# FFN pairs: a fixed matmul order, sums of weight blocks on GpSimd, and two more wide pairs

## The chip, the cores and the metric

The kernel runs on one core of one Trainium2 chip. The metric is the device time of one execution in microseconds; the times shown are those of separate runs. The profile is taken in an execution of its own, and its span goes from the first to the last instruction of the program.

In the profile PE is TensorE (matmuls), PEld its loads of the stationary operand, DVE is VectorE, ACT ScalarE, POOL GpSimd and SP SyncE (which issues DMAs). A line such as L410 is line 410 of the kernel.

## The reference

One layer of an encoder over 512 tokens of width 1024: a half-step SwiGLU FFN, a mixing stage of two attention branches, and a second half-step FFN. Each has an RMSNorm before and after it. All of it is in float32.

```python
def _swiglu(x, w_gate, w_up, w_down):
    return (jax.nn.silu(x @ w_gate) * (x @ w_up)) @ w_down

f = _swiglu(_rmsnorm(x, ffn1_pre_g[l]), ffn1_w_gate[l], ffn1_w_up[l], ffn1_w_down[l])
x = x + 0.5 * _rmsnorm(f, ffn1_post_g[l])
...
f = _swiglu(_rmsnorm(x, ffn2_pre_g[l]), ffn2_w_gate[l], ffn2_w_up[l], ffn2_w_down[l])
x = x + 0.5 * _rmsnorm(f, ffn2_post_g[l])
```

The hidden width of an FFN is 2816, that is 22 tiles of 128 features (`NF = 22`). Only the two FFNs are touched by the change.

## The kernel before

**Precision.** A float32 product is made of three matmuls in the faster type float32r. Each operand is split into a high part (a cast on ACT, L113) and a low part (what is left, a subtraction on DVE, L114); high x high, high x low and low x high are added in PSUM (`mm3`, L204 to L206).

**Pairs.** An FFN works through its 22 hidden tiles in order. Each is a pair: a gate product and an up product of the normed input with a block of weights. The first two pairs (`STD`) are done in the plain way (`proj_into`). The other 20 go through `seven`, a Strassen-like scheme with seven block products instead of eight. The 1024 input features and the 512 tokens are both cut in halves, and gate and up weights take the place of the second dimension of blocks. So each pair j has seven products, numbered 1 to 7, of a block of weights 128 features wide with 256 tokens. The tokens' side (`mv`) is formed once for an FFN by `combined`; the weights' side is formed for each pair.

**Blocks of weights.** `load_blocks` issues a pair's loads: on SP plain ones, on GpSimd's queue two that add in the DMA (t1, which is up + gate, at L404, and t3 at L405). `sums_of` then forms two more blocks: t2 = t1 + w11 (L410), and t4 from t2 and another block (L412 for the first four pairs, which have it loaded, L415 for the others). `split_block` splits a block into high and low. `ready(j + 1, i)` calls these for the next pair between the products of this one, and past the last pair it takes steps of the down projection instead (`lead`, and `far` through `get`). The first four pairs (`EARLY`) have their products 1 and 2 done ahead, in `first_products`.

**One turn of the loop** over j (L485 on), as written: product 1 of pair j into a bank q; then 7 of pair j - 1 (q) and 5 of pair j (p); then 2 (r) and 6 (q) of pair j, 4 of pair j - 1 (q) and 3 of pair j (p). Between them ACT copies a bank before it is added to again (L494 after product 1, L514 after 5, L523 after 6, L527 after 7 and 4) and DVE combines the copies with later sums (L505 and L506 for 7 less 5, L520 for product 2, L528, L535 and L536), until `use7` forms silu(gate) x up (L636, L645, L646).

**Wide products.** In a narrow product each of the four blocks of 128 input features takes three matmuls over 256 tokens (`mm3`). In a wide one the tokens' high and low parts lie side by side, so the weights' high part is multiplied with both at once in one matmul over 512 columns (L461), and the low part with the high tokens over 256 (L464). The two halves of the 512 columns must then be added, so the copies and sums behind it work on 512 columns, or are one more. `run` issues the first halves (L461) of all products of a group and then their second halves (L464). Which pairs may be wide is `state["wide"]`: in the first FFN pairs 4 to 17 of 0 to 19, in the second all. Product 1 is narrow in every pair, and in the first four pairs only 5 and 3 can be wide.

**What sets the order.** The kernel is built through a planner, which simulates the engines and gives each engine a fixed list; dependences, written order and priorities go into it. So the order on an engine need not be the written one. Where the code wants the written order it says so: at the end of `block_kernel` a loop goes over ranges of the program (`ordered` for PE, ACT and DVE together, `pool` with the engines named in each entry) and chains all instructions of an engine in a range. The pair loop was in no such range for PE. The down projection (`rest`) chains GpSimd's instructions from its start on.

**Rooms.** Blocks and sums live in 38 rooms of 128 x 512 (`unit`), split blocks in 12 of 128 x 1024 (`wp`), PSUM results in 8 banks. A load waits until its room is free.

Of the kernel before, what the change touches and what calls it, by code (L numbers as in the profile page):

```python
# [16 lines left out]
ALU = mybir.AluOpType  # L17
# [7 lines left out]
NF = 2816 // P  # L25
# [10 lines left out]
STD = 2  # L36
# [10 lines left out]
def block_kernel(ctx, tc, x, gains, weights, rpb_near, rpb_all, alibi0, alibi12, out):  # L47
    nc = tc.nc
# [12 lines left out]
    def unit(dt=F32, name="u"):  # L61
        return up.tile([P, 512], dt, tag="u", name=name)
# [57 lines left out]
    state = {"used": False, "next": 0, "take": 0, "stop": EARLY + 2 * STD, "ahead": lambda: None}  # L120
    ordered = []
    pool = []
# [65 lines left out]
    def mark():  # L188
        return len(nc.cur_bb.bb.instructions)
# [199 lines left out]
    def load_blocks(n0, j):  # L389

        w11, t1, t3 = unit(name="w11"), unit(name="t1"), unit(name="t3")
        gate, up = (n0 + j, n0 + EARLY + 2 * STD + j) if j < EARLY else [n0 + 2 * STD + 2 * j + i for i in range(2)]
        nc.sync.dma_start(t1, weights[up][:, :512])
        nc.sync.dma_start(t3, weights[up][:, :512])
        raw = {3: w11, 5: t1, 7: t3}
        if j < EARLY:
            raw[4] = unit(name="t4")
            nc.sync.dma_start(raw[4], weights[gate][:, 512:])
        else:
            r = wp.tile([P, PIECE], F32, tag="raw", name="raw", bufs=2)  # L400
            nc.sync.dma_start(r, weights[gate])
            raw[1], raw[2] = r[:, :512], r[:, 512:]
        nc.sync.dma_start(w11, weights[up][:, 512:])
        nc.gpsimd.dma_start(t1, weights[gate][:, :512], accum_op=ALU.add)  # L404
        nc.gpsimd.dma_start(t3, weights[up][:, 512:], accum_op=ALU.add)  # L405
        return raw

    def sums_of(raw):
        raw[6] = unit(name="t2")
        nc.vector.tensor_tensor(raw[6], raw[5], raw[3], op=ALU.add)  # L410
        if 4 in raw:
            nc.vector.tensor_tensor(raw[4], raw[6], raw[4], op=ALU.add)  # L412
        else:
            raw[4] = unit(name="t4")
            nc.vector.tensor_tensor(raw[4], raw[6], raw[2], op=ALU.add)  # L415

    def split_block(raw):
        w = wp.tile([P, PIECE], F32R, tag="w", name="w")
        split(w[:, :512], w[:, 512:], raw)
        return w  # L420

    def seven(use, mv, n_pairs, n0, behind, far, lead, raws, early, put, pin):

        blocks = {}
        o = {}

        def get(j):
            if j < n_pairs and j > 2:
                raws[j] = load_blocks(n0, j)
            if j >= n_pairs - 1:
                behind(far)

        def ready(j, i):
            if j < n_pairs:
                if j and loads:
                    loads.popleft()()  # L440
                if i == 1:
                    sums_of(raws[j])
                if j >= EARLY or i not in (1, 2):
                    blocks[j, i] = split_block(raws[j].pop(i))
            else:
                behind(lead)

        def product(j, i, key, start):
            if start:
                o[key, j] = bank(key)  # L450
            w = blocks.pop((j, i))
            high = [w[:, k * P:(k + 1) * P] for k in range(4)]
            low = [w[:, 512 + k * P:512 + (k + 1) * P] for k in range(4)]
            acc = o[key, j][:, :256]
            if i not in WIDE or j not in state["wide"] or (key in "qr" and j < EARLY):
                for k in range(4):
                    mm3(acc, high[k], low[k], *mv[i][k][:2], start and k == 0, k == 3, skip_group_check=True)
                return
            for k in range(4):
                to = shaped(o[key, j], mv[i][k][2])  # L460
                nc.tensor.matmul(to, high[k], mv[i][k][2], start=start and k == 0, stop=False, skip_group_check=True)  # L461
            yield
            for k in range(4):
                nc.tensor.matmul(acc, low[k], mv[i][k][0], start=False, stop=k == 3, skip_group_check=True)  # L464

        def run(*products):
            products = [product(*p) for p in products]
            for _ in range(2):
                for p in products:
                    next(p, None)  # L470

        def full(j):
            return j in state["wide"] and j >= EARLY

        res = {}
        get(0)
        get(1)
        blocks[0, 5] = split_block(raws[0][5])
        ready(0, 1)
        raws[0].pop(5)  # L480
        for i in (6, 3, 7, 4):
            ready(0, i)
            if i == 3:
                put()
        for j in range(n_pairs + 1):  # L485
            now, was = j < n_pairs, j > 0
            get(j + 2)
            if now:
                if j < EARLY:
                    o["q", j], g = early[j]  # L490
                else:
                    run((j, 1, "q", True))
                    g = unit(name="g")
                    nc.scalar.copy(g[:, :256], o["q", j][:, :256])  # L494
                u = unit(name="up")
                res[j] = g, u, unit(name="p5") if j in state["wide"] else u[:, 256:]
            ready(j + 1, 1)
            if pin and j == 0:
                pool.append((pin, mark(), (mybir.EngineType.DVE,)))
            run(*[(j - 1, 7, "q", False)] * was, *[(j, 5, "p", True)] * now)  # L500
            if was:
                g0, u0, s0 = res.pop(j - 1)
                q0 = o["q", j - 1]
                if full(j - 1):
                    nc.vector.tensor_tensor(s0, s0, q0, op=ALU.subtract)  # L505
                    nc.vector.tensor_tensor(u0[:, 256:], s0[:, :256], s0[:, 256:], op=ALU.add)  # L506
                else:
                    nc.vector.tensor_tensor(u0[:, 256:], s0[:, :256], q0[:, :256], op=ALU.subtract)
                if j - 1 in state["wide"] and not full(j - 1):
                    nc.vector.tensor_tensor(u0[:, 256:], u0[:, 256:], s0[:, 256:], op=ALU.add)  # L510
            ready(j + 1, 5)
            if now:
                p = o["p", j]
                nc.scalar.copy(res[j][2], p if j in state["wide"] else p[:, :256])  # L514
            ready(j + 1, 2)
            two = now and j >= EARLY
            run(*[(j, 2, "r", True)] * two, *[(j, 6, "q", False)] * now, *[(j - 1, 4, "q", False)] * was, *[(j, 3, "p", False)] * now)
            if two:
                for part in range(1 + full(j)):
                    nc.vector.tensor_tensor(g[:, :256], g[:, :256], o["r", j][:, part * 256:part * 256 + 256], op=ALU.add)  # L520
            ready(j + 1, 6)
            if now:
                nc.scalar.copy(u if full(j) else u[:, :256], o["q", j] if full(j) else o["q", j][:, :256])  # L523
            ready(j + 1, 3)
            if was:
                if full(j - 1):
                    nc.scalar.copy(g0[:, 256:], q0[:, 256:])  # L527
                    nc.vector.tensor_tensor(g0[:, 256:], q0[:, :256], g0[:, 256:], op=ALU.add)  # L528
                    use(j - 1, g0, u0, g0[:, 256:])
                else:  # L530
                    use(j - 1, g0, u0, q0[:, :256])
            ready(j + 1, 7)
            if now:
                if full(j):
                    nc.vector.tensor_tensor(u, p, u, op=ALU.subtract)  # L535
                    nc.vector.tensor_tensor(u[:, :256], u[:, :256], u[:, 256:], op=ALU.add)  # L536
                else:
                    nc.vector.tensor_tensor(u[:, :256], p[:, :256], u[:, :256], op=ALU.subtract)
                if j in state["wide"] and not full(j):
                    nc.vector.tensor_tensor(u[:, :256], p[:, 256:], u[:, :256], op=ALU.add)  # L540
            ready(j + 1, 4)

    def first_of_next():
        return [n for n in sorted(spread) if n >= state["next"]][:SPREAD]
# [72 lines left out]
    def ffn(g, store, src):  # L617
# [31 lines left out]
        raws = {}  # L649
# [27 lines left out]

        far, lead, rest = down(m, after, duos, hidden, g_post, g_pre, store, src)
        state["next"] = state["take"] = after + 2 * m + 2
        state["wide"] = range(NF - STD) if store else range(4, NF - STD - 2)  # L680
        seven(use7, mv, NF - STD, n0, lambda q: [f() for f in q.popleft()], far, lead, raws, early, put, pin)
        rest()

# [869 lines left out]
    raws = []  # L1553
# [9 lines left out]
    for n in range(2, 4):  # L1563
        raw = wp.tile([P, PIECE], F32, tag="raw", name="raw", bufs=2)
# [233 lines left out]
```

## Time and profile before

| | us |
|---|---|
| median of 3 runs | 1072.0 |
| lowest and highest run | 1071.46, 1072.08 |
| the profiled execution | 1071.59 |
| its span | 1069.8 |

| stage, by the timeline | us from the span's start |
|---|---|
| pairs of the first FFN (`seven`) | about 40 to 232 |
| down projection of the first FFN | about 225 to 339 |
| mixing stage | about 339 to 740 |
| pairs of the second FFN | about 766 to 963 |
| down projection of the second FFN and the output | about 951 to 1070 |

The page's first part has each engine's busy time, its share of the span and its instructions. The windows view gives each engine's busy time in a stretch (with the number of instructions), the clock granted to PE and the load of the DMA engines. The timeline lists one engine's instructions: start, duration, then in brackets the idle time before it and what ended that. The groups by line give busy time in all, mean ns of one, and idle time before them.

### The profile page before, as it was taken

The page shows a single profiled execution, that of the slowest core. Times are in us where ns is not written, and L with a number is a line of the kernel's source. Part 1 is how long each engine was busy: PE and PEld are TensorE (multiplying, and loading weights), DVE is VectorE, ACT ScalarE, POOL GpSimd, SP SyncE. Part 2 cuts the span into 40 slices and gives each one's busy share as a digit, 9 for nine tenths or more (in the row PEclk, how much of TensorE's full clock was granted, in tenths as well). Part 3 has the DMA queues.
Part 4 walks back from the last instruction along what each step waited for, and adds up shares of the span by engine and source line. Part 5 has one row for each costly group of instructions (what it writes and reads, how often), then busy time and mean ns, then how long its engine had stood idle before and what let it go on. Part 6 is the DMA issues. An engine that isn't in the chain of part 4 may idle for free.

```text
span 1069.8 us, 17141 instructions
## 1 busy us (share of the span) xinstructions
PE 1060.3 (99%) x5939; PEld 924.1 (86%) x5939; DVE 871.1 (81%) x1698; ACT 655.1 (61%) x1348; POOL 191.2 (18%) x253
## 2 busy tenths in 40 slices
PE   9999999999999999999999999999999999999997
PEld 7899888998888988888988888889899888887886
DVE  7989999989987566777777644777999989999985
ACT  7656657576684665567766641366656556667671
POOL 4112111124334000000000001143301111123321
PEclk9999999999999999999999999999999999999999
DMA  9889988779993444322232239585938767869952
GB/s 338 190 218 239 228 196 214 197 182 269 255 305 112 164 162 148 118 79 60 81 104 81 79 126 300 150 198 192 285 81 206 175 180 197 210 208 229 219 197 79
DMA packets 98026, 193.95 MB, mean 181 GB/s; under 512 B 24337, under 2 KB 26897, under 8 KB 97938
## 3 DMA queue, kind: packets, MB, share of 16 engines
q1 hardware_dynamic: 69760, 138.37, 38.8%
q0 software_dynamic: 25488, 54.01, 28.1%
q8 instruction: 47, 0.77, 0.3%
q10 hardware_dynamic: 2690, 0.46, 0.2%
q14 instruction: 41, 0.34, 0.1%
HBM read 185.68 MB, written 9.68 MB: 183 GB/s over the span
## 4 chain that ended last, share of the span: by engine, by line
PE 98%; DVE 1%; issue 0%; ACT 0%; DVEq 0%; ACTq 0%
PE ps L204 11%; PE ps L206 11%; PE ps L205 11%; PE q L461 8%; PE q L206 7%; PE q L205 7%; PE q L204 7%; PE p L461 6%; PE q L464 4%; PE p L464 3%; PE r L461 3%; PE c L205 2%; PE c L204 2%; PE c L206 2%; PE q L270 1%; PE r L464 1%
## 5 line engine op out<-in xcount | busy, mean ns | idle before, releaser
L114 DVE TENSOR_TENSOR w<-raw,w 128x512 fp32r<-128x512 f32 (+1 forms) x142 | 129.9, 919 | 73.7 <-ACT w L113 71.0
L113 ACT CAST w<-raw 128x512 fp32r<-128x512 f32 (+1 forms) x142 | 113.9, 808 | 81.8 <-PE ps L205 32.0
L204 PE MATMUL ps<-hn,w 128*128 128x512 f32 (+1 forms) x360 | 136.6, 379 | 0.0
L206 PE MATMUL ps<-hn,w 128*128 128x512 f32 (+1 forms) x360 | 134.5, 374 | 0.0
L205 PE MATMUL ps<-hn,w 128*128 128x512 f32 (+1 forms) x360 | 134.3, 373 | 0.0
L113 ACT CAST w<-t 128x512 fp32r<-128x512 f32 x160 | 96.0, 622 | 58.5 <-DVE t L410 44.9
L114 DVE TENSOR_TENSOR w<-t,w 128x512 fp32r<-128x512 f32 x160 | 106.6, 684 | 1.6 <-ACT w L113 1.5
L404 POOL DMA_DIRECT2D t<-in_weights_dram x40 | 35.0, 874 | 288.2 <-DVE w L114 89.3
L206 PEld LDWEIGHTS ps<-hn,w 128*128 128x128 f32 x360 | 67.8, 188 | 12.7 <-DVE w L114 0.6
L204 PEld LDWEIGHTS ps<-hn,w 128*128 128x128 f32 x360 | 67.8, 188 | 11.4
L205 PEld LDWEIGHTS ps<-hn,w 128*128 128x128 f32 x360 | 67.9, 189 | 10.9
L461 PE MATMUL p<-v,w 128*128 128x512 f32 x272 | 75.6, 394 | 0.0
L113 ACT CAST w<-room 128x1024 fp32r<-128x1024 f32 x49 | 51.5, 1053 | 36.0 <-PE q L206 7.4
L114 DVE TENSOR_TENSOR w<-room,w 128x1024 fp32r<-128x1024 f32 x49 | 59.6, 1219 | 7.1 <-ACT w L113 3.2
L461 PE MATMUL q<-v,w 128*128 128x512 f32 x240 | 65.3, 393 | 0.0
L748 POOL DMA_DIRECT2D room<-in_weights_dram x7 | 6.1, 872 | 320.5 <-DMA room<-in_weights_dram 319.6
L729 POOL DMA_DIRECT2D rows<-in_weights_dram x36 | 35.2, 1242 | 96.1 <-DVE w L114 91.7
L461 PEld LDWEIGHTS p<-v,w 128*128 128x128 f32 x272 | 47.0, 189 | 6.2
L205 PE MATMUL q<-hn,w 128*128 128x256 f32 x168 | 47.5, 282 | 0.0
L206 PE MATMUL q<-hn,w 128*128 128x256 f32 x168 | 47.4, 282 | 0.0
L204 PE MATMUL q<-hn,w 128*128 128x256 f32 x168 | 47.4, 282 | 0.0
L113 ACT CAST w<-rows 128x512 fp32r<-128x512 f32 x62 | 35.7, 619 | 18.6 <-PE q L206 6.7
(334 smaller groups left out, 3055.7 us busy)
## 6 DMA issues: line engine op xcount, KB each, us to landing
raw<-in_weights_dram SPq DMA_DIRECT2D x94, 512.0 KB
t<-in_weights_dram SPq DMA_DIRECT2D x88, 256.0 KB
t<-in_weights_dram POOLq DMA_DIRECT2D x80, 256.0 KB, 6.1
room<-in_weights_dram SPq DMA_DIRECT2D x37, 512.0 KB
room<-in_weights_dram POOLq DMA_DIRECT2D x29, 512.0 KB, 12.1
w<-in_weights_dram SPq DMA_DIRECT2D x40, 256.0 KB
rows<-in_weights_dram POOLq DMA_DIRECT2D x36, 256.0 KB, 8.6
w<-in_weights_dram POOLq DMA_DIRECT2D x32, 256.0 KB, 7.6
```

The source lines that it names most:

```text
L113: nc.scalar.copy(hi, src)
L114: nc.vector.tensor_tensor(lo, src, hi.bitcast(F32), op=ALU.subtract)
L204: nc.tensor.matmul(o, sh, mh, start=start, stop=False, **kw)
L205: nc.tensor.matmul(o, sh, ml, start=False, stop=False, **kw)
L206: nc.tensor.matmul(o, sl, mh, start=False, stop=stop, **kw)
L270: nc.tensor.matmul(to, parts[j][part], hn_hi[:, k0 + j, 0:256], start=k0 + j + part == 0, stop=False, skip_group_check=True)
L404: nc.gpsimd.dma_start(t1, weights[gate][:, :512], accum_op=ALU.add)
L461: nc.tensor.matmul(to, high[k], mv[i][k][2], start=start and k == 0, stop=False, skip_group_check=True)
L464: nc.tensor.matmul(acc, low[k], mv[i][k][0], start=False, stop=k == 3, skip_group_check=True)
L729: nc.gpsimd.dma_start(u, block(*add, d)[:, cs], accum_op=ALU.add)
L748: nc.gpsimd.dma_start(to, self.block(*b, 0), accum_op=ALU.add)
```

## The change

Three edits. `sums_of` takes the engine as an argument: for pairs 0 to 2 it stays VectorE, from pair 3 on it is GpSimd. The loop over the pairs becomes a range in which PE's instructions are chained as written. And in the first FFN the last two pairs, 18 and 19, may be wide too.

```diff
-    def sums_of(raw):
+    def sums_of(raw, engine):
         raw[6] = unit(name="t2")
-        nc.vector.tensor_tensor(raw[6], raw[5], raw[3], op=ALU.add)
+        engine.tensor_tensor(raw[6], raw[5], raw[3], op=ALU.add)
         if 4 in raw:
-            nc.vector.tensor_tensor(raw[4], raw[6], raw[4], op=ALU.add)
+            engine.tensor_tensor(raw[4], raw[6], raw[4], op=ALU.add)
         else:
             raw[4] = unit(name="t4")
-            nc.vector.tensor_tensor(raw[4], raw[6], raw[2], op=ALU.add)
+            engine.tensor_tensor(raw[4], raw[6], raw[2], op=ALU.add)
...
                 if i == 1:
-                    sums_of(raws[j])
+                    sums_of(raws[j], nc.vector if j < 3 else nc.gpsimd)
...
             if i == 3:
                 put()
+        begin = mark()
         for j in range(n_pairs + 1):
             now, was = j < n_pairs, j > 0
             get(j + 2)
...
             ready(j + 1, 4)
+        pool.append((begin, mark(), (mybir.EngineType.PE,)))
...
         state["next"] = state["take"] = after + 2 * m + 2
-        state["wide"] = range(NF - STD) if store else range(4, NF - STD - 2)
+        state["wide"] = range(NF - STD) if store else range(4, NF - STD)
```

## The prediction

> **What bounds the kernel now.** I read the page's head first, then the windows view over the pair loops, then the timeline of PE, and only then the other engines.
>
> ```profile
> span 1069.8 us, 17141 instructions
> PE 1060.3 (99%) x5939; PEld 924.1 (86%) x5939; DVE 871.1 (81%) x1698; ACT 655.1 (61%) x1348; POOL 191.2 (18%) x253
> ...
> PEclk9999999999999999999999999999999999999999
> ...
> PE 98%; DVE 1%; issue 0%; ACT 0%; DVEq 0%; ACTq 0%
> ```
>
> PE is busy for 1060.3 of 1069.8 us at full granted clock, and 98% of the chain that ended last is PE. All idle time of PE together is 9.5 us, start and end of the kernel included. So whatever is taken from DVE pays only where PE waits for DVE, and PE's own work is the thing to count. The windows view shows the same in the loops (columns: busy us of each engine, clock, DMA share, GB/s):
>
> ```profile
> core 0: us, PE busy (x) PEld busy (x) DVE busy (x) ACT busy (x) POOL busy (x), PEclk, DMA share, GB/s
> 120.00:160.00 40.00, 40.00 (x245) 35.74 (x244) 36.66 (x73) 24.69 (x54) 7.16 (x9) 1.00 0.85 208
> 160.00:200.00 40.00, 40.00 (x246) 35.77 (x245) 37.04 (x74) 25.09 (x54) 8.78 (x10) 1.00 0.87 204
> 200.00:240.00 40.00, 40.00 (x274) 37.08 (x273) 35.51 (x66) 27.46 (x58) 7.13 (x8) 1.00 0.68 190
> 240.00:280.00 40.00, 40.00 (x178) 33.12 (x177) 39.91 (x63) 26.34 (x44) 17.82 (x20) 1.00 1.07 251
> 940.00:980.00 40.00, 39.03 (x197) 32.60 (x197) 38.33 (x68) 28.01 (x53) 10.07 (x12) 1.00 0.88 237
> ```
>
> In the middle of the first FFN's pairs (120 to 200) PE has no idle time, though DVE is busy 92% of it. Only where the second FFN's pairs run into its down projection (940 to 980) does PE lose about 1 us. The two losses in the timeline of PE:
>
> ```profile
> 960.80 0.39 PE L206 MATMUL r<-w,a 128*128 128x512 f32 x1
> 961.41 1.19 PE L461 MATMUL q<-hn,w 128*128 128x512 f32 x4 [0.22 <-DVE p L505]
> ...
> 963.61 0.39 PE L205 MATMUL q<-w,a 128*128 128x512 f32 x1
> 964.76 0.50 PE L206 MATMUL q<-w,a 128*128 128x512 f32 x1 [0.75 <-DVE a L114]
> ```
>
> A duration in it overlaps the next matmul, so I count from start to start. 960.80 to 961.41 is 0.61 us and 963.61 to 964.76 is 1.15, where the neighbours are about 0.23 apart: 0.38 + 0.92 = 1.3 us lost to a late DVE.
>
> **The wide pairs.** What a wide product saves is read from the same view:
>
> ```profile
> 127.48 1.07 PE L461 MATMUL q<-v,w 128*128 128x512 f32 x4
> 128.39 0.64 PE L464 MATMUL q<-v,w 128*128 128x256 f32 x4
> ...
> 182.75 1.09 PE L461 MATMUL p<-v,w 128*128 128x512 f32 x4
> 183.68 0.63 PE L464 MATMUL p<-v,w 128*128 128x256 f32 x4
> 184.15 0.28 PE L204 MATMUL q<-hn,w 128*128 128x256 f32 x1
> ...
> 185.58 1.09 PE L461 MATMUL p<-v,w 128*128 128x512 f32 x4
> ...
> 203.83 0.28 PE L204 MATMUL q<-hn,w 128*128 128x256 f32 x1
> ```
>
> A wide product is 0.93 + 0.47 = 1.40 us (182.75 to 184.15). A narrow one, twelve matmuls, is 1.43 (184.15 to 185.58). Fewer instructions, but nearly the same columns per second: 0.03 us each. Pairs 18 and 19 of the first FFN have six products each that turn wide (5, 2, 6, 3, 7, 4), so 12 x 0.03 = **0.4 us saved** on PE, and since PE is the bound there, it counts in full unless DVE falls behind.
>
> The price is on DVE, whose steps are in its timeline:
>
> ```profile
> 117.80 0.68 DVE L410 TENSOR_TENSOR t<-t,w 128x512 f32<-128x512 f32 x1
> 118.40 0.42 DVE L520 TENSOR_TENSOR g<-g,r 128x256 f32<-128x256 f32 x1
> 118.73 0.68 DVE L415 TENSOR_TENSOR t<-t,raw 128x512 f32<-128x512 f32 x1
> 119.34 0.41 DVE L520 TENSOR_TENSOR g<-g,r 128x256 f32<-128x256 f32 x1
> 119.67 0.68 DVE L114 TENSOR_TENSOR w<-t,w 128x512 fp32r<-128x512 f32 x1
> ```
>
> Back to back, a 512-wide operation takes 0.6 us and a 256-wide one 0.33. By the code a wide pair has one L520 more (0.33), L505 and L506 for L508 (0.6), L528 (0.33), and L535 and L536 for L538 (0.6): some 1.9 us, 3.7 for both pairs. Moving their sums takes 2 x 2 x 0.6 = 2.4 off. DVE has 4.5 us free in 200 to 240, so it comes out at 35.5 + 3.7 - 2.4 = 36.8 of 40, but the next window is already full (39.91), with no room for a backlog. The second FFN has its last pairs wide already, and lost 1.3 us there. I charge the first FFN 0.3 for this (bounds 0 and 1.3).
>
> **The sums.** L410 and L415 leave DVE for pairs 3 to 19 of both FFNs: 34 x 2 x 0.6 = 41 us of DVE work. In the middle of the loops that buys nothing, since PE waits for nothing there. At 940 to 980 it frees 2.4 us for pairs 18 and 19 just ahead of the two late operations, more than the 1.3 us lost. I take **0.9 of the 1.3**, since the waits move to the next late thing on DVE (bounds 0 and 1.3).
>
> On GpSimd the nearest row is L1612 (groups by line), an operation of the same shape on two SBUF operands; the timelines of POOL and DVE then show how GpSimd's reading fares beside DVE:
>
> ```profile
> L1612 POOL TENSOR_TENSOR w<-raw,w 128x512 fp32r<-128x512 f32 x2 | 2.6, 1294 | 2.7 <-ACT w L1611 2.7
> L300 POOL TENSOR_SCALAR ms<-ssx 128x1 f32<-128x1 f32 x10 | 3.2, 318 | 17.8 <-ACT junk L292 17.8
> ```
>
> ```profile
> 1026.47 6.31 POOL L300 TENSOR_SCALAR ms<-ssf 128x1 f32<-128x1 f32 x1 [18.22 <-ACT pair L113]
> ```
>
> ```profile
> 1032.02 0.68 DVE L114 TENSOR_TENSOR pair<-v,pair 128x512 fp32r<-128x512 f32 x1
> 1033.08 0.69 DVE L114 TENSOR_TENSOR w<-rows,w 128x512 fp32r<-128x512 f32 x1 [0.38 <-ACT w L113]
> ```
>
> Two sums are 2 x 1.29 = 2.6 us of GpSimd's 9.84 us per pair (184.15 to 203.83 is two pairs). That fits: in 120 to 160 it is busy 7.2 of 40. But the L300 that began at 1026.47, 0.32 us on the mean otherwise, took 6.31 and ended at 1032.78, just after DVE's unbroken run of additions from SBUF stopped at 1032.70. A GpSimd operation that reads SBUF waits while DVE reads two SBUF operands. Whether DVE waits in turn for a long GpSimd operation no row shows. Bounds: 0 (DVE never waits) and 2.6 us per pair (it waits through both sums). Against 1.2 us taken off, that is -1.2 to +1.4 us of DVE per pair. I take half of 2.6, so DVE stays near the 9.1 us per pair that it has now (73.7 busy of 80 us): no relief, and no harm.
>
> The Trainium skill ("SBUF — State Buffer", section "Who interferes with whom") states that a DVE instruction with two SBUF inputs and a GpSimd instruction that reads SBUF exclude each other, and that the second to start waits for all of the first. The row of 6.31 us agrees for GpSimd as the waiter. By that rule DVE waits too: the 0.9 us taken above would fall away and the sum would be 1071.9; its full effect is the second rival.
>
> How late may a sum be? The timelines of POOL and of ACT, and the page's DMA issues (its last column is us to landing):
>
> ```profile
> 104.23 0.87 POOL L404 DMA_DIRECT2D t<-in_weights_dram  x1 [6.80 <-DMA t<-in_weights_dram]
> ...
> 113.83 0.87 POOL L405 DMA_DIRECT2D t<-in_weights_dram  x1
> 121.22 0.87 POOL L404 DMA_DIRECT2D t<-in_weights_dram  x1 [6.52 <-DVE w L114]
> ```
>
> ```profile
> 126.81 0.62 ACT L113 CAST w<-t 128x512 fp32r<-128x512 f32 x1 [2.08 <-DVE t L410]
> 127.33 0.58 ACT L514 COPY p<-p 128x512 f32<-128x512 f32 x1
> ```
>
> ```profile
> t<-in_weights_dram POOLq DMA_DIRECT2D x80, 256.0 KB, 6.1
> ```
>
> The accumulation issued at 104.23 lands some 6 us later, at 110; DVE forms its sum only at 117.80. GpSimd is free from 114.7 (L405 at 113.83) to 121.2, so both sums fit there even at twice their length, and the next L404 isn't held up. If they are late, ACT's cast waits, with the copy L514 queued behind it, and PE's product 3 waits for that copy.
>
> **The order as written.** It adds no instruction. It takes from PE the freedom to run something else while an operand is late. By the code 5 and 7 end together; then come the first halves of 2, 6, 4 and 3. Product 4 needs L505, which needs product 7: between them lie 0.47 (5's second half) and 2 x 0.93, so 2.3 us for an operation of 0.68. Product 3 needs the copy L514 (0.58) and has 3 x 0.93 = 2.8. Both are enough if DVE and ACT come to them within 1.6 and 2.2 us, two or three operations. I take 0 for it (bounds: -4.0 and +5, from the first and the last rival); the down projection's products are outside the order and still fill the end of the loop.
>
> **Sum.** The profiled execution took 1071.59 us (span 1069.8, and 1.8 around it). -0.4 (wide) +0.3 (DVE at the first FFN's end) -0.9 (second FFN's end) = -1.0: 1070.6. The median of the runs, 1072.0, is 0.4 above the profiled one; that gives **1071.0**. About 0.2% (2.1 us) is what a measurement of this kernel can tell from no change, so this is "no change": 1069.9 to 1074.1.
>
> **Rivals.**
>
> *Steps on PE get shorter (chance 0.22, about 1068.3).* The product at 127.48 took 0.91 for its four wide steps where the one at 182.75 took 0.93. I don't see in the trace what decides this. If the order decides it, 188 wide products of now (14 x 6 in the first FFN, 16 x 6 + 4 x 2 in the second) and 12 new ones gain up to 200 x 0.02 = 4.0 us. Half of that with all 1.3 us of the stalls and the 0.4 is -3.7 from 1072.0. For it: PE is the bound, so each step counts. Against it: slow products occur in every order that the trace has.
>
> *DVE waits for GpSimd and becomes the bound (0.14).* DVE has 9.06 - 1.2 = 7.9 us of its own per pair. It decides the time once GpSimd's reads block it for more than 9.84 - 7.9 = 1.9 of their 2.6 us. At the full 2.6 it has 10.5, 0.66 over PE's 9.84: 34 x 0.66 = 22 us, 1093; half-way over the point 11 us, 1082. For it: the row of 6.31 us, and most of DVE's operations in a pair read two SBUF operands. Against it: L505, L520, L528 and L535 read PSUM, and DVE has gaps in which a sum can start.
>
> *A late copy or sum stalls PE in its fixed order (0.14, about 1076).* If L505 or L514 comes 0.15 us too late in each of 34 pairs, that is 5 us. For it: DVE is over 90% busy, and the planner's order now leaves far more room:
>
> ```profile
> 130.27 0.64 PE L464 MATMUL p<-v,w 128*128 128x256 f32 x4
> ```
>
> ```profile
> 139.04 0.58 ACT L514 COPY p<-p 128x512 f32<-128x512 f32 x1
> ```
>
> Product 5 ends at 130.74 and is copied 8.3 us later, since it runs almost a pair ahead of product 3; as written it has 2.8. Against it: the planner places DVE's and ACT's work anew around the fixed order, and a stall that happens once shifts the phase and is not paid again.
>
> **How the numbers follow.** Forecast 0.50, shorter steps 0.22, DVE bound 0.14, late copies 0.14. So faster by over 0.2%: 0.22; within: 0.50; slower: 0.28. The range, 1067.8 to 1081, takes in the forecast's band, most of the first rival, the late copies and the lower part of the DVE case; it leaves out about 0.12.
>
> **What would show it.** Right: PE without idle time in the pair windows; wide products in the first FFN's last pairs at 1.40 us; the waits for L505 and for the down projection's cast at the end of the second FFN shorter; L410 and L415 on POOL at 1.3 us or, where DVE runs unbroken, more; DVE's busy time per pair about 1.2 lower with waits of DVE in its place. Wrong: PE waiting for L505, L514 or L523 in many pairs (late copies), DVE near 40 of 40 with PE idle (DVE bound), or wide products nearer 1.38 than 1.40 (shorter steps). A change elsewhere, in the mixing stage, by which the planner's new order moves the time, would make it wrong too; no row speaks for that.

## The result and the profile after

| | before | after |
|---|---|---|
| median of 6 runs each, us | 1071.83 | 1104.71 |
| lowest and highest run | 1071.46, 1072.08 | 1100.81, 1109.0 |
| the profiled execution | 1071.59 | 1100.81 |
| its span | 1069.8 | 1098.6 |

The ratio is 1.0308, with a 95% interval of 1.0285 to 1.0331. The changed kernel is some 33 us slower. The lines of its code stand one or two lower: L494 is now L495, L505 L506, L506 L507, L514 L515, L520 L521, L528 L529, L535 L536, L636 L638.

The head and the chain of work of the changed kernel's page:

```profile
span 1098.6 us, 17150 instructions
...
PE 1069.5 (97%) x5891; PEld 922.8 (84%) x5891; DVE 907.2 (83%) x1638; ACT 654.2 (60%) x1350; POOL 284.9 (26%) x321
...
PE 74%; DVE 15%; DMA 5%; issue 3%; ACT 2%; SPq 1%; DVEq 0%; POOL 0%; ACTq 0%
```

PE carried 98% of the chain and carries 74% now; DVE has 15%. And DVE is busy for 36 us more than before (907.2 against 871.1) with 60 instructions fewer, though 68 sums, at 0.6 us each, were taken from it. Its remaining instructions must have become longer.

PE's idle time grew from 9.5 to 29.1 us (span less busy). The rest of the longer span, 9.2 us, is in PE's own busy time (1069.5 against 1060.3), though it has 48 matmuls fewer: matmuls next to a wait are recorded longer. The half of product 4 that waits in the pair shown below takes 1.03 us from start to start, against 0.91 in the same place of e4. These 9.2 us were not followed further.

The windows view of the changed kernel (columns as before):

```profile
120.00:160.00 40.00, 38.44 (x234) 33.69 (x233) 39.48 (x62) 22.60 (x50) 18.99 (x18) 1.00 0.80 207
160.00:200.00 40.00, 38.94 (x236) 34.30 (x235) 39.86 (x62) 23.13 (x50) 16.39 (x15) 1.00 0.73 192
780.00:820.00 40.00, 36.52 (x247) 33.87 (x246) 37.41 (x58) 19.83 (x41) 14.90 (x13) 0.96 0.48 111
820.00:860.00 40.00, 36.91 (x223) 32.16 (x222) 38.03 (x58) 22.83 (x49) 18.15 (x16) 1.00 0.69 162
860.00:900.00 40.00, 36.78 (x222) 32.14 (x223) 36.68 (x57) 21.31 (x46) 16.80 (x15) 1.00 0.72 177
900.00:940.00 40.00, 34.20 (x201) 28.99 (x199) 37.93 (x58) 20.67 (x46) 15.36 (x13) 1.00 0.61 155
940.00:980.00 40.00, 40.00 (x243) 35.87 (x244) 37.53 (x66) 25.14 (x52) 10.65 (x10) 1.00 0.63 183
```

In the first FFN DVE is full (39.5 and 39.9 of 40) and PE loses 1.1 to 1.6 us of each 40. In the second FFN, up to 940 us, PE loses 3 to 6 of each 40 while DVE is *not* full (36.7 to 38.0): there the two engines wait for each other. From 940 to 980 PE loses nothing. What PE waits for in the pairs, from the waits view (us in all, times, the longest), is nearly always the same:

```profile
PE q L461 <- DVE p L506: 15.7, 18, 1.7
PE q L204 <- DVE up L509: 3.8, 3, 3.2
```

That is product 4, which waits for DVE's subtraction L506, the operand that the prediction gave 2.3 us of time; L509 is the same step in the first four pairs. Why DVE is late is shown by the groups by line, in 82 to 200 us. First the changed kernel:

```profile
L114 DVE TENSOR_TENSOR w<-t,w 128x512 fp32r<-128x512 f32 x47 | 45.7, 973 | 0.3 <-ACT w L113 0.3
L114 DVE TENSOR_TENSOR w<-raw,w 128x512 fp32r<-128x512 f32 x23 | 17.8, 773 | 0.0
L507 DVE TENSOR_TENSOR up<-p 128x256 f32<-128x256 f32 x11 | 11.6, 1050 | 0.2
L638 DVE TENSOR_TENSOR h<-up,g 128x256 f32<-128x256 f32 x22 | 10.9, 515 | 0.0
L521 DVE TENSOR_TENSOR g<-g,r 128x256 f32<-128x256 f32 x24 | 9.9, 411 | 0.2
L114 DVE TENSOR_TENSOR w<-w,w 128x512 fp32r<-128x512 f32 x11 | 9.5, 867 | 0.0
...
L506 DVE TENSOR_TENSOR p<-p,q 128x512 f32<-128x512 f32 x11 | 7.4, 676 | 0.0
```

And the same view of e4 (below: the changed kernel with its sums back on DVE), for the groups that differ:

```profile
L114 DVE TENSOR_TENSOR w<-t,w 128x512 fp32r<-128x512 f32 x48 | 32.9, 685 | 0.0
L114 DVE TENSOR_TENSOR w<-raw,w 128x512 fp32r<-128x512 f32 x24 | 16.4, 684 | 0.1
...
L638 DVE TENSOR_TENSOR h<-up,g 128x256 f32<-128x256 f32 x23 | 9.1, 418 | 0.0
...
L114 DVE TENSOR_TENSOR w<-w,w 128x512 fp32r<-128x512 f32 x12 | 8.3, 689 | 1.2 <-ACT w L113 1.2
...
L507 DVE TENSOR_TENSOR up<-p 128x256 f32<-128x256 f32 x12 | 5.0, 418 | 0.0
```

Operations with two operands in SBUF are longer (L114, L507, L638, and L537 in the pair below); those with one in PSUM are not (L521 411 ns, L506 676 ns). The surplus is 47 x 0.288 + 23 x 0.089 + 11 x 0.632 + 22 x 0.097 + 11 x 0.178 = 26.6 us. With 11 to 12 pairs in the window that is some **2.3 us per pair**, for two sums. DVE's own work without the sums is 7.7 us per pair (its instructions of twelve pairs, each at its undisturbed step), so it needs 10.0 where PE needs 9.84.

One pair of the second FFN shows how a stretch comes about (timeline of the changed kernel, DVE, then POOL, then PE):

```profile
873.60 0.42 DVE L521 TENSOR_TENSOR g<-g,r 128x256 f32<-128x256 f32 x1 [1.14 <-PE r L464]
...
874.61 2.12 DVE L114 TENSOR_TENSOR w<-t,w 128x512 fp32r<-128x512 f32 x1
876.65 0.68 DVE L536 TENSOR_TENSOR up<-p,up 128x512 f32<-128x512 f32 x1
...
878.78 1.51 DVE L537 TENSOR_TENSOR up<-up 128x256 f32<-128x256 f32 x1
...
881.49 0.68 DVE L506 TENSOR_TENSOR p<-p,q 128x512 f32<-128x512 f32 x1
...
884.84 0.88 DVE L521 TENSOR_TENSOR g<-g,r 128x256 f32<-128x256 f32 x2 [0.42 <-PE r L464]
```

```profile
874.57 1.59 POOL L415 TENSOR_TENSOR t<-t,raw 128x512 f32<-128x512 f32 x1
...
878.36 1.65 POOL L410 TENSOR_TENSOR t<-t,w 128x512 f32<-128x512 f32 x1 [1.36 <-DVE g L529]
```

```profile
882.22 1.20 PE L461 MATMUL q<-hn,w 128*128 128x512 f32 x4 [1.14 <-DVE p L506]
```

The sum L415 began at 874.57 and ended at 876.16. The subtraction L114 came 0.04 us after it and ended at 876.73, 0.57 after the sum, which is about its full step of 0.6: it did next to nothing while the sum ran. L537 met the second sum, which ended at 880.01, and ended at 880.29. The Trainium skill ("SBUF — State Buffer", section "Who interferes with whom") says that the instruction that comes second waits for the whole of the first; the two rows agree with it.

Now count round the pair. From L521's start (873.60) to the end of L506 (881.49 + 0.68 = 882.17) DVE needs 8.57, of which 1.43 and 1.10 are stretch (2.12 against 0.69, 1.51 against 0.41). Product 4 starts 0.05 later, and its half, that of product 3 and the second half of product 2 run until L521 can start again, at 884.84, 2.62 later. 8.57 + 0.05 + 2.62 = **11.24 us** from one L521 to the next, with PE idle for 1.14. The pairs are a ring: DVE's next section waits for product 2, which stands behind product 4, which waits for DVE's last section.

### The profile page after: what moved, and what is told of

It reads as the page before. It is cut to its first block, busy times and chain, and to the rows that moved or that the text cites. A ratio compares the mean times of both kernels' runs of the same rounds, so it can differ in the third digit from the quotient of the medians.

```text
span 1098.6 us, 17150 instructions
## 1 busy us (share of the span) xinstructions
PE 1069.5 (97%) x5891; PEld 922.8 (84%) x5891; DVE 907.2 (83%) x1638; ACT 654.2 (60%) x1350; POOL 284.9 (26%) x321
## 4 chain that ended last, share of the span: by engine, by line
PE 74%; DVE 15%; DMA 5%; issue 3%; ACT 2%; SPq 1%; DVEq 0%; POOL 0%; ACTq 0%
PE ps L204 10%; PE ps L205 10%; PE ps L206 10%; DVE w L114 7%; PE q L206 5%; PE q L204 5%; PE q L205 5%; PE q L461 4%; PE p L461 3%; PE c L205 2%; PE c L204 2%; PE c L206 2%; DVE h L638 2%; DMA raw<-in_weights_dram 2%; PE q L464 2%
## 5 line engine op out<-in xcount | busy, mean ns | idle before, releaser
L114 DVE TENSOR_TENSOR w<-raw,w 128x512 fp32r<-128x512 f32 (+1 forms) x142 | 138.3, 979 | 74.8 <-ACT w L113 71.4
L113 ACT CAST w<-raw 128x512 fp32r<-128x512 f32 (+1 forms) x142 | 114.0, 809 | 83.0 <-PE ps L205 32.1
L113 ACT CAST w<-t 128x512 fp32r<-128x512 f32 x160 | 98.6, 622 | 93.2 <-PE r L464 74.2
L114 DVE TENSOR_TENSOR w<-t,w 128x512 fp32r<-128x512 f32 x160 | 146.2, 920 | 2.0 <-ACT w L113 2.0
L461 PE MATMUL p<-v,w 128*128 128x512 f32 x288 | 77.9, 392 | 0.0
L204 PEld LDWEIGHTS ps<-hn,w 128*128 128x128 f32 x360 | 67.9, 189 | 11.4
L410 POOL TENSOR_TENSOR t<-t,w 128x512 f32<-128x512 f32 x34 | 51.9, 1526 | 74.5 <-DVE w L114 33.1
L461 PE MATMUL q<-v,w 128*128 128x512 f32 x256 | 69.4, 393 | 0.4 <-ACT g L495 0.4
L113 ACT CAST w<-room 128x1024 fp32r<-128x1024 f32 x49 | 51.5, 1054 | 26.3 <-PE ps L205 5.2
L114 DVE TENSOR_TENSOR w<-room,w 128x1024 fp32r<-128x1024 f32 x49 | 60.1, 1233 | 5.6 <-ACT w L113 3.8
L461 PEld LDWEIGHTS p<-v,w 128*128 128x128 f32 x288 | 53.7, 189 | 11.3
L461 PEld LDWEIGHTS q<-v,w 128*128 128x128 f32 x256 | 46.1, 189 | 9.1 <-ACT g L495 0.8
L461 PE MATMUL q<-hn,w 128*128 128x512 f32 x128 | 37.0, 410 | 16.0 <-DVE p L506 15.7
L415 POOL TENSOR_TENSOR t<-t,raw 128x512 f32<-128x512 f32 x32 | 52.3, 1635 | 0.4
## 6 DMA issues: line engine op xcount, KB each, us to landing
room<-in_weights_dram POOLq DMA_DIRECT2D x29, 512.0 KB, 11.2
```

Of the source, the lines that this page charges most:

```text
L113: nc.scalar.copy(hi, src)
L114: nc.vector.tensor_tensor(lo, src, hi.bitcast(F32), op=ALU.subtract)
L204: nc.tensor.matmul(o, sh, mh, start=start, stop=False, **kw)
L410: engine.tensor_tensor(raw[6], raw[5], raw[3], op=ALU.add)
L415: engine.tensor_tensor(raw[4], raw[6], raw[2], op=ALU.add)
```

## The experiments

The time between the end of the subtraction that product 4 needs and that product's start is what I call its room. Where a kernel's stage is given, "second FFN" is the time from its first wide product to its last, from the timeline.

### The three edits, alone and in pairs

e1 has the sums on GpSimd and nothing else of the change:

```diff
-                    sums_of(raws[j])
+                    sums_of(raws[j], nc.vector if j < 3 else nc.gpsimd)
```

> The kernel before with the sums of pairs 3 to 19 on GpSimd and nothing else of the change. Theory A (each GpSimd sum holds up VectorE's additions from SBUF, so that VectorE becomes the bound): the trace after shows 73 us of stretched VectorE operations for 68 sums, 2.2 us per pair, against 1.2 us taken off; so nearly the whole loss comes from here: 1095 to 1107 us, VectorE near 40 of 40 in the windows of the pairs and its splits (L114) stretched to some 0.9 us and more. Theory B (the loss comes from PE's fixed order, in which a late copy or sum can't be passed by): 1070 to 1076 us.

Measured: 1076.99 us, ratio 1.0049 (1.0032 to 1.0067), so 5.2 us slower. That is outside both ranges, 1 us above theory B's; theory A, by which nearly the whole loss comes from the sums, fell. The stretch is there all the same: DVE is busy for 897.6 us against 871.1 with 68 sums fewer, so 26.5 + 68 x 0.6 = 67 us of it, for a sixth of the loss. The same count gives 36 + 41 - 4 = 73 us in the changed kernel, where the wide pairs' 4 us are taken off.

e2 has the order as written and nothing else:

```diff
+        begin = mark()
         for j in range(n_pairs + 1):
...
+        pool.append((begin, mark(), (mybir.EngineType.PE,)))
```

> The kernel before with PE's order in the pair loop chained as written and nothing else. Theory A: VectorE keeps its 9.1 us per pair under PE's 9.84, so PE seldom waits: 1070 to 1076 us. Theory B: PE waits for L505 and the copies in many pairs: 1085 us or more, with PE waiting for the combination after product 7 as in the trace after.

Measured: 1070.98 us, ratio 0.9992 (0.9983 to 1.0001): no change, so theory B fell for the order by itself.

e3 has the wide pairs alone (`range(4, NF - STD)`), e4 the order and the wide pairs, with the sums on DVE:

> The kernel before with pairs 18 and 19 of the first FFN wide and nothing else. Both theories: 12 products at 0.03 us less make 0.4 us; VectorE gets 3.7 us more work there and may lose up to 1.3 us at the end of the loop, as in the second FFN: 1071 to 1073 us.

> The changed kernel with the sums back on VectorE: order as written, wide last pairs. Theory A: back to the kernel before within a few us, 1070 to 1077. Theory B: most of the loss stays, 1085 us or more.

Measured: e3 1073.08 us, 1.0011 (1.0002 to 1.0021), just above its range; e4 1072.25 us, 1.0003 (0.9994 to 1.0012), as theory A had it: without the sums on GpSimd the loss is gone.

x2 has the sums and the order, without the wide pairs:

> Sums on GpSimd and PE's order as written, without the wide last pairs. All theories but one: the loss is that of the two edits together, 1098 to 1110 us. If the wide pairs take part: below 1090.

Measured: 1102.71 us, 1.0289 (1.0271 to 1.0308).

What follows: the wide pairs have no part in the loss that these runs can tell (x2 is 2.0 us below the changed kernel, and the intervals overlap). The sums cost 5.2 us by themselves, the order -0.8, and both together 30.9. So some 26 us come from the two **meeting**, and no edit's own price holds them.

The trace of e4 tells what the order does to the room. Its timeline, DVE then PE, in the place shown above for the changed kernel:

```profile
874.34 0.42 DVE L521 TENSOR_TENSOR g<-g,r 128x256 f32<-128x256 f32 x1 [0.85 <-PE r L464]
...
879.68 0.68 DVE L506 TENSOR_TENSOR p<-p,q 128x512 f32<-128x512 f32 x1
...
884.14 0.87 DVE L521 TENSOR_TENSOR g<-g,r 128x256 f32<-128x256 f32 x2
```

```profile
881.65 1.07 PE L461 MATMUL q<-hn,w 128*128 128x512 f32 x4
```

DVE's section takes 879.68 + 0.68 - 874.34 = 6.02 us, then 1.29 us of room, then 2.49 on PE: 9.80 in all, one pair of PE's work. In the kernel before, where the planner placed the products, the room was (DVE, then PE):

```profile
874.47 0.68 DVE L505 TENSOR_TENSOR p<-p,q 128x512 f32<-128x512 f32 x1
...
881.29 0.69 DVE L505 TENSOR_TENSOR p<-p,q 128x512 f32<-128x512 f32 x1 [0.24 <-PE q L464]
```

```profile
878.28 1.09 PE L461 MATMUL q<-hn,w 128*128 128x512 f32 x4
...
884.86 1.07 PE L461 MATMUL q<-hn,w 128*128 128x512 f32 x4
```

that is 878.28 - 875.15 = 3.1 and 884.86 - 881.98 = 2.9 us. Over all pairs of the traces it is 2.8 to 4.3 before (but for the last pair), 1.1 to 1.3 in most pairs of e4, and 0.32 or less in 26 of 32 pairs of the changed kernel. A stretch of 2.5 us fits into the room of the free order and not into that of the fixed one: 6.02 + 2.53 + 0.05 + 2.62 = 11.2.

### Half of the sums

e7 is the changed kernel with the sum L410 back on DVE; L415 stays on GpSimd:

```diff
-        engine.tensor_tensor(raw[6], raw[5], raw[3], op=ALU.add)
+        nc.vector.tensor_tensor(raw[6], raw[5], raw[3], op=ALU.add)
```

> The changed kernel with the first sum (L410) back on VectorE and the second on GpSimd. VectorE has 9.06 - 0.6 + 1.05 = 9.5 us per pair, under PE's 9.84. Theory C: the ring has up to 0.7 us of VectorE's idle time on top, 10.2: half of the loss or less, 1072 to 1088 us. Theory D: half of the loss, 1085 to 1092.

Measured: 1077.54 us, 1.0046 (1.0029 to 1.0062). Half of the sums bring 5.8 of 33 us: the price isn't proportional. Theory C's range holds this time, theory D's does not. The stretch is 30.2 us in all here, counted as each operation's surplus over its ordinary length, so 0.9 us for each of 34 pairs. That fits into the room of 1.1 to 1.3, and DVE's 8.3 us of its own and 0.9 stay under PE's 9.84. Where the 5.8 us come from was not followed; PE's waits for L506 are 2.4 us of them.

### Is it GpSimd's reading, or that GpSimd is slow?

e6 is the kernel before, with six fills by GpSimd of the room into which DVE then writes its first sum. They only write; they read nothing:

```diff
         raw[6] = unit(name="t2")
+        if fill:
+            for _ in range(6):
+                nc.gpsimd.memset(raw[6], 0.0)
```

> The kernel before, with VectorE's sums kept, and six fills of 128x512 by GpSimd ahead of the first sum of each pair from 3 on, in that sum's room: about 2.9 us of GpSimd per pair that write and read nothing. If GpSimd's reading is what holds up VectorE: no VectorE operation stretched, 1071 to 1074 us. If any work of GpSimd holds it up: some 2 us per pair on top of 9.06, so 1100 us and more.

Measured: 1101.2 us, 1.0267 (1.0249 to 1.0285). The group of fills, the group that was stretched (in 82 to 200 us), and what PE waited for:

```profile
L412 POOL MEMSET t<- 128x512 f32 x204 | 133.1, 671 | 31.7 <-DVE w L114 19.2 <-DVE h L639 6.1
```

```profile
L114 DVE TENSOR_TENSOR w<-t,w 128x512 fp32r<-128x512 f32 x44 | 29.8, 687 | 0.2
```

```profile
PE p L464 <- ACT p L517: 16.3, 11, 2.2
```

133 us of GpSimd's writes stretched no operation of DVE (687 ns). Yet the time rose, by another way: DVE's first sum had to wait for the fills, ACT's cast waited for the sum, and ACT's copy for PE stood behind the cast. So the time is in the range for "any work of GpSimd", and for another reason than that one. That was a fault of the experiment: it asked about the stretch and added a wait. It does show that a sum that is late by itself can cost as much.

m1 mends it: the changed kernel, where each sum on GpSimd becomes a 128x1 addition of the same inputs and two fills of its room. The sums themselves are left out, so it doesn't compute the layer. GpSimd reads next to nothing, but takes 3.7 us for a pair by the group means, against 3.2 in the changed kernel, so its results come no earlier.

```diff
-        engine.tensor_tensor(raw[6], raw[5], raw[3], op=ALU.add)
...
+            engine.tensor_tensor(raw[6][:, :1], raw[5][:, :1], raw[3][:, :1], op=ALU.add)
+            for _ in range(2):
+                engine.memset(raw[6], 0.0)
...
```

> The changed kernel, in which each of GpSimd's 512-wide sums of FFN pairs 3 and on is replaced by a 128x1 add of the same inputs and two fills of its room: GpSimd is as busy and sums come no earlier, but it reads next to nothing. The sums are left out of the computation. Theory A (GpSimd's reading stretches VectorE's two-operand operations by some 73 us in all, and the fixed order can't take that up): the stretch goes, and the time comes to 1075 us or less. Theory B (the sums merely come late from a slow engine, whose queue holds ScalarE's and VectorE's up): 1090 us or more, with the stretch gone. Between the two, both share it.

Measured: 1074.19 us, 1.0027 (1.0018 to 1.0037). Its windows view and the group in 82 to 200 us:

```profile
120.00:160.00 40.00, 40.00 (x245) 35.91 (x244) 32.37 (x65) 23.94 (x52) 20.97 (x36) 1.00 0.85 222
```

```profile
L114 DVE TENSOR_TENSOR w<-t,w 128x512 fp32r<-128x512 f32 x47 | 32.2, 686 | 3.1 <-ACT w L113 3.1
```

GpSimd is even busier than in the changed kernel (20.97 of 40 us against 18.99), the order is the same, and 30 of the 33 us are gone. So theory A holds: the loss needs the stretch of DVE's operations by GpSimd's reading, and a slow GpSimd alone doesn't make it.

### Is it the ring, or DVE's load?

x1 runs product 2 alone, ahead of the group, so that DVE's next section doesn't stand behind product 4; x3 puts product 4 last; x4 does both (products by their numbers):

```diff
-            run(2, 6, 4, 3)
+            run(2); run(6, 4, 3)        # x1
+            run(2, 6, 3, 4)             # x3
+            run(2); run(6, 3); run(4)   # x4
```

> The changed kernel with product 2 run alone, both halves, ahead of the group of 6, 4 and 3. Theory C (a ring: the combination after product 7 on VectorE comes late behind stretched operations; product 4 waits for it, the second half of product 2 stands behind the first halves of 4 and 3 in the fixed order, and VectorE's next addition and ScalarE's next cast wait for that half, so VectorE is idle while it is the bound): the ring is cut, VectorE needs about 9.06 - 1.2 + 2.1 = 9.95 us per pair against PE's 9.84, so 1074 to 1084 us. Theory D (the throughput of VectorE and GpSimd on the shared reading is itself worse in this order; waits on PE are only its echo): 1095 us or more.

> The changed kernel with one step of the fixed order moved: product 4, which waits for VectorE's late operation of the same pair, stands last in its group (2, 6, 3, 4 in place of 2, 6, 4, 3), so that this operation has some 0.9 us more. If the loss is VectorE's late operation waited for by product 4: about 0.9 us per pair where PE now waits 1.2 to 1.7, over 24 to 34 pairs, so 1075 to 1088 us. If what counts is the ring (VectorE's next pair starts on PE's last product, and product 4 waits for VectorE): the delay is passed on and the time stays at 1097 to 1106 us.

> The changed kernel, whose group of four products is split into three that run one after another: 2 alone, then 6 with 3, then 4 alone. Product 4, which waits for VectorE's late operation of its pair, then stands ahead of neither product 2, on which VectorE's next section starts, nor 6 or 3. Ring theory (the late operation, product 4, the rest of the group, and VectorE's next section in a circle, each waiting for the one before): the circle is open, and what is left is VectorE's throughput, some 10.0 us per pair against 9.85, as with the sums alone: 1075 to 1082 us. Load theory (VectorE's load with any fixed order): no better than with one of the two steps moved, 1093 to 1100 us.

| | us, ratio (interval) | second FFN, us | PE waits for L506 | PE waits for the copy L515 |
|---|---|---|---|---|
| e4, sums on DVE | 1072.25, 1.0003 (0.9994 to 1.0012) | 197.8 | 0.9 | none |
| changed kernel | 1104.71, 1.0308 (1.0285 to 1.0331) | 218.8 | 15.7 | none |
| x1 | 1097.52, 1.0240 (1.0211 to 1.0268) | 215.2 | 11.6 | none |
| x3 | 1097.68, 1.0244 (1.0230 to 1.0258) | 215.1 | 0.6 | 12.3 |
| x4 | 1099.88, 1.0268 (1.0253 to 1.0284) | 211.1 | none | 15.2 |

x1 fell: cutting the ring behind product 2 should have given 1074 to 1084 us, and the time is in theory D's range. x3 is in the range of the ring theory, but PE hardly waits for L506 there; it waits for the copy L515 instead. My expectation for x4 fell too. The time is the one that it gave for the load theory. The wait for L506 is gone and the second FFN is 7.7 us shorter, as the ring theory had it, but the first FFN's last product ends 7.9 us later (254.1 against 246.2 us from the start), and PE now waits for the copy L515, above all near the start of the FFNs. The timeline of x4 there, DVE, ACT, then PE:

```profile
792.37 5.40 DVE L114 TENSOR_TENSOR w<-t,w 128x512 fp32r<-128x512 f32 x3
797.70 0.68 DVE L410 TENSOR_TENSOR t<-t,w 128x512 f32<-128x512 f32 x1
```

```profile
798.41 0.62 ACT L113 CAST w<-t 128x512 fp32r<-128x512 f32 x1 [8.62 <-DVE t L410]
...
799.97 0.58 ACT L515 COPY p<-p 128x512 f32<-128x512 f32 x1
```

```profile
800.60 2.08 PE L461 MATMUL p<-v,w 128*128 128x512 f32 x4 [5.56 <-ACT p L515]
```

Three subtractions that take 1.9 us undisturbed (2 steps of 0.6 and one of 0.69) took 5.40, beside two sums of GpSimd. The sum behind them (one of a pair that stays on DVE) came late, ACT's cast waited 8.6 us for it, the copy stood behind the cast, and PE's product behind the copy.

So did the ring matter at all? In the middle of the second FFN, where it was found, it did. Between 820 and 940 us PE is idle for 12.1 us in the changed kernel, 6.8 in x1, 2.6 in x3 and 2.7 in x4. In return it is idle for 3.2 us between 82 and 200 in the changed kernel, but for 6.0 in x1, 5.0 in x3 and 8.6 in x4. One window of x4, to be set beside the changed kernel's with 36.91:

```profile
820.00:860.00 40.00, 39.26 (x247) 35.00 (x246) 38.90 (x58) 21.75 (x46) 17.64 (x16) 1.00 0.67 174
```

The ring is one form of the loss; opened, the loss finds the next operand with little room. No run here gives every operand room, so that room is all that is missing is argued, not shown.

m2 asks whether DVE's load is enough, without GpSimd: all sums on DVE, and per pair two more additions whose result nobody reads, in the fixed order with its wide pairs. m3 is the same load in the free order.

```diff
+        for _ in range(2 * (engine is nc.gpsimd)):
+            junk = sp.tile([P, 512], BF16, tag="junk", name="junk", bufs=1)
+            nc.vector.tensor_tensor(junk, raw[5], raw[3], op=ALU.add)
```

> The changed kernel with all sums back on VectorE, and two further 512-wide adds of VectorE per pair from pair 3 on, whose result nobody reads: VectorE has about 8.98 + 2 x 0.6 = 10.2 us per pair by itself, as much as it had with the stretch (7.73 + 2.4), but spread as the queue's planner places it, and GpSimd adds nothing. If VectorE's load alone decides, in a fixed order: as late as the changed kernel, 1095 to 1105 us. If only the surplus over the 9.8 us of PE counts: 0.35 us x 34 pairs = 12 us, so 1080 to 1085 us; the remainder of the loss is then from where the stretch falls, which is the piece of VectorE's queue between the copy of the result and the operation that PE waits for.

> The kernel before (free order, sums on VectorE) with the same two further adds of VectorE per pair as in the run above that had them in the fixed order (1097.6 us). If VectorE's load of 10.2 us per pair is simply above PE's 9.85 us: as late as in the fixed order, 1090 to 1100 us, and the order matters only where stretch and order meet. If the fixed order is what turns load into loss: 1074 to 1082 us.

Measured: m2 1097.61 us, 1.0246 (1.0231 to 1.0262); m3 1086.19 us, 1.0132 (1.0116 to 1.0147). m2 is in the range for load alone, above the one for the bare surplus. A window of the second FFN, m2 then m3:

```profile
860.00:900.00 40.00, 38.80 (x235) 34.17 (x236) 38.94 (x78) 23.31 (x50) 6.98 (x8) 1.00 0.69 178
```

```profile
860.00:900.00 40.00, 39.62 (x238) 34.71 (x236) 39.76 (x79) 23.47 (x52) 7.00 (x8) 1.00 0.68 179
```

Not every window shows the difference: from 820 to 860 PE is busy for 38.96 us in m2 and 38.71 in m3. Over the whole span PE is idle for 24.3 us in m2 and 17.1 in m3.

Neither theory had m3 right; it lies between. 10.2 us of DVE's own work per pair cost 14.4 us in the free order, near the bare surplus of 34 x (10.2 - 9.84) = 12 us. The fixed order, with the wide pairs (1.2 by themselves in e3), adds 11.4 to that. So stretch isn't needed once DVE is over its limit: the same rule, that the fixed order pays more than the surplus, holds for plain load too. In the changed kernel DVE's load is a little smaller (10.0 to 10.2) and the loss larger.

### A better version

b1 is the kernel before with the order fixed and product 2 alone, b2 with the group split as in x4; the sums stay on DVE.

> The kernel before with the matmul order fixed and product 2 run alone ahead of the group of 6, 4 and 3; sums stay on VectorE, nothing is wide. The order alone gave 1070.98 us (ratio 0.9992). If the operation that waits for product 2 is late in that order: some tenths of a us on 34 pairs, 1066 to 1069 us. If nothing waits there with the sums on VectorE, as PE's step excess near zero says: 1070 to 1073 us.

> The kernel before with the order fixed and the group split in the same three steps, sums on VectorE: nothing waits in the fixed order there, so splitting gives nothing or takes a few tenths per pair out of PE's way: 1069 to 1072 us. If split products cost PE time of their own (one product's high and low parts follow each other on one bank): 1074 us or more.

Measured: b1 1070.65 us, 0.9989 (0.9980 to 0.9998); b2 1072.71 us, 1.0008 (0.9999 to 1.0016). b1 is the fastest kernel of the study, by 0.1%; its interval just leaves out 1, and 0.1% is less than the prediction took as telling from no change. b2 is 0.7 us above its range. Splitting products costs next to nothing where DVE has room, so x1 and x4 are not slow from the split itself.

## Why the prediction was wrong

**PE as the bound** was right for the kernel before and for e2 and e4.

**The wide pairs** were put at -0.4 + 0.3 = -0.1. e3 shows +0.2 to +2.3 us. The charge for the first FFN's end was too small; its upper bound of 1.3 gives +0.9, which agrees. But it was charged for DVE, and in e3 PE waits once at that end, 0.73 us at 238.61, for a cast on ACT (L113). That DVE is behind it is not shown.

**The 1.3 us at the end of the second FFN** went as forecast: in e1 PE has no wait between 940 and 985 us, and in the changed kernel one of 0.5 us at the end of the loop. It is lost in the rest.

**The step that failed first**: "I take half of 2.6, so DVE stays near the 9.1 us per pair that it has now (73.7 busy of 80 us): no relief, and no harm." Two sums took 1.53 + 1.64 = 3.2 us on GpSimd (group means), not 2.6; that they too wait for DVE where they come second would explain it:

```profile
L410 POOL TENSOR_TENSOR t<-t,w 128x512 f32<-128x512 f32 x34 | 51.9, 1526 | 74.5 <-DVE w L114 33.1
...
L415 POOL TENSOR_TENSOR t<-t,raw 128x512 f32<-128x512 f32 x32 | 52.3, 1635 | 0.4
```

They held DVE up for 2.3 us per pair, past the point of 1.9 that the second rival had named. By that rival's way of counting, with 7.7 us of DVE's own work in place of its 7.9, the price would be 34 x (7.7 + 2.3 - 9.84) = 5 us. The sums alone cost 5.2. So the mechanism of that rival was right, and the value taken was the wrong one. That the price agrees so well is partly luck: with its own 7.9 the same sum gives 12 us. Nor is e1's loss spread over the pairs. Two waits for L505 in the first FFN, at 113.54 and 144.73 us, make 3.8 us of it, and between 820 and 940 us PE is idle for 0.2. What spoke against it, that DVE has gaps in which a sum can start, was no help. In the middle of e1's pairs DVE has hardly any left (its windows view; the first line has one of the two waits):

```profile
120.00:160.00 40.00, 37.44 (x224) 32.89 (x223) 38.96 (x54) 22.06 (x48) 20.06 (x17) 1.00 0.85 215
160.00:200.00 40.00, 40.00 (x243) 35.43 (x242) 39.93 (x70) 24.12 (x53) 17.81 (x16) 1.00 0.78 202
820.00:860.00 40.00, 40.00 (x245) 35.72 (x244) 39.90 (x66) 25.20 (x54) 21.65 (x17) 1.00 0.78 198
```

**The step that failed second**, and cost more: on the order as written, "I take 0 for it (bounds: -4.0 and +5, from the first and the last rival)". Alone it is 0 (e2). But the 0 stood on DVE being as punctual as it is with its sums at home. The prediction counted 2.3 us for product 4's operand, 1.6 of them to spare; e4 shows 1.1 to 1.3. Even the half of 2.6 that it charged for the sums, 1.3, would have used all of that up, and the step on the order never took that number in. Each edit was priced against the kernel before, and the prices were added. Even the measured prices, -0.8, +1.2 and +5.2 (e2, e3, e1), add up to +5.6 only, and the change measures +33.

The third rival had the place, L505 before product 4, but not the size: it put the delay at 0.15 us per pair. And its counter-argument, "a stall that happens once shifts the phase and is not paid again", is refuted by the 18 waits for L506: the stall is paid again and again. In the ring of 11.24 us this is so because DVE's next section starts on a product behind the stalled one; x3 and x4 bear that out for the middle of the second FFN, and nothing here shows it for the rest. The two rivals were set down as alternatives; what happened is both at once.

**What was right beside it**: GpSimd had the time for the sums (busy for 15 to 19 of 40 us in the windows shown above, up to 940), and the signs named for being wrong, PE waiting for L505 in many pairs and DVE near 40 of 40 with PE idle, are the ones that came.

**What stays open.** The 26 us of the meeting are not split further. From e4 to the changed kernel 21.0 us arose in the second FFN (197.8 to 218.8) and 7.3 up to the first FFN's last product (238.9 to 246.2 us from the start), though the stretch is 32 us in the first and 41 in the second (each operation's surplus over its ordinary length, from the timeline). The sums alone (e1) lengthen the second FFN by only 1.8 us, from 196.9 to 198.7, so most of the meeting is there. Why the ring closes in the second and less in the first was not tried. Nor was a fixed order with more room for every operand at once.

## What to carry to other kernels

Before work is moved to GpSimd beside a VectorE as full as here (92% busy in the pairs), count VectorE's operations with two SBUF operands and charge nearly the whole length of the GpSimd operation to VectorE, not half of it. Here two sums that take 2.6 us alone added 2.3 us per pair, and saved 1.2. Price edits of one change against each other: an order that is fixed is free only as long as every operand's lateness stays inside the room that the order leaves, so read that room (end of the operand to start of its user, pair by pair) and compare it with what the other edits add. When a wait goes and the time stays, look for the next operand in the same queue before the theory is given up, and also before it is kept.

## What was not expected of the hardware

One GpSimd sum of 128x512 held a two-operand VectorE operation for 1.1 to 1.4 us in the pair shown (1.43 and 1.10), while operations with an operand in PSUM kept their full speed in the group means (676 and 411 ns). Fills of the same size, 204 of them, held up none.

In the changed kernel's window of 780 to 820 us the granted clock is 0.96; the page's slices show nothing of it. In windows of 5 us it is 0.66 from 790 to 795, right behind PE's longest wait, 3.17 us, and 1.00 in the others. In x4 it is 0.61 from 800 to 805, behind the wait of 5.56 us, and the half of a product there takes 1.88 us from start to start, where 0.91 is usual. Behind the changed kernel's waits of up to 1.71 us the 40 us windows keep 1.00. At most 4% of 40 us, 1.6 us, hang on it in the changed kernel. That the wait brings the drop about was not tried.
